# Two PSUM bank pairs of a hybrid encoder, each given to one part of the scan, and the bonus sums moved beside the key sums

## The chip, the cores and the metric

One core of a Trainium2 chip runs the whole program. The metric is the device time of one execution in microseconds (us). Engines are called by the names of the profile: PE (TensorE, matmuls), PEld (its weight loads), DVE (VectorE), ACT (ScalarE), POOL (GpSimd), SP (SyncE, which issues the DMAs). Each engine works through a queue of its own in order and meets the others at semaphores.

## The reference

Two encoder layers on 256 tokens of width 2048. Each projects its normed input to two groups of heads: 16 RWKV-7 heads of 64 (a delta-rule scan in both directions) and a windowed attention. Both are gated, joined, sent through an output projection and added to the residual. The change lies in the scan, of which this matters here:

```
kk = heads(k * k_k);  kk = kk * rsqrt(max(sum(kk * kk), 1e-24))     # sum over a head's 64: "key sums"
for d in (forward, reverse):
    decay = exp(-exp(-softplus(-(w0[d] + tanh(xw) @ decay_up[d])) - 0.5))
    a     = sigmoid(a0[d] + xa @ iclr_up[d])
    kd    = heads(k * (1 + (a - 1) * k_a))
    y     = y + wkv_scan(r, decay, kd, v, kk, a, reverse=d)
    bonus = bonus + sum(r * kd * r_k)                                # over a head's 64: "bonus sums"
out = norm(y) * lnx_g + lnx_b + bonus * v
```

`wkv_scan` steps a 64 by 64 state S over the tokens: S = S * decay - (S kk)(a kk) + v kd, output S r.

## The kernel before

**Tiling.** The 256 tokens lie in the free dimension, features on the 128 partitions; one scan step takes two heads (128 partitions) at a time, so there are 8 head pairs p in each layer. A projection tile `pm` (128 output columns by 256 tokens) sums 16 steps of contraction; each step is three matmuls, since fp32 weights and inputs are split into a high and a low part (L311 hi by high `XH`, L312 hi by low `XL`, L313 `lo` by high). ACT makes `hi` from the raw weights (L241), DVE makes `lo` (L243), SP loads them. The projections of both layers form one long stream of such steps on PE.

**Windows and slots.** The rest of the work is cut into Python generators, which the kernel runs in windows. A window has 64 projection steps in 11 slots (`SLOTS`); in each slot some generators go one `yield` further, and then PE gets that slot's projection steps. Window w holds the work of several head pairs at once: `scan_p` prepares p = w and p = w - 1, `scan_i` (the Gram products `pg` and a triangular solve by doubling: `pq`, `pd`, with `tt` and `tv` the parts of the inverse) works on p = w - 2 and w - 3, `scan_b` (the chunk recurrence `pcc`, `suv`, and the output `py`, normed to `ysq` and turned back by PE at L1043) on w - 3 and w - 4. `STAGE_P`, `STAGE_I` and `STAGE_B` list for each lag the slots in which a generator is taken on; the first half of `STAGE_P` is for p = w, the second for p = w - 1, and each half has the steps at the front of a slot (`[8]`, `[9]`) and those behind the other scans.

**What sets the order.** PE's order is the order of the program. On the other engines a scheduler places instructions by priority; those called through `PA` and `PV` stay in program order among themselves on ACT and DVE, whose remaining instructions it moves between them (`lo` gets a priority of its own, `scan_b` another). A wait of PE holds all the projection steps behind it.

**`scan_p`.** It squares the keys (`mf`, `sl` are high and low parts of the squares), sums them over each head by a matmul with `BONES` into `pk`, and keeps the sums as `kd` (ACT). `pza` (L691 to L693) is the low-rank product of decay and rate; ACT takes `th` and `FR` from it, and DVE prefix sums and products follow (`FR`, `pp`, `ip`, `kd` with the reciprocal, `th`, `mv`). The bonus is `km` (shown as `th`), split into high and low (`ip`), summed by `BONES` into `pbn` (L706), and multiplied with v to `bv` on DVE.

**PSUM.** 8 banks of 512 fp32 columns. `ps_main` holds two projection tiles, `ps_c` the recurrence's tiles, and `ps_w` two pairs of banks under one tag, "w". A `wpair(name)` takes the next pair in turn, and its first writer waits until the readers of the tile that had that pair before are done. All of `pk`, `pza`, `vt`, `pbn`, `pg`, `pt`, `pq`, `pd`, `pf`, `pn`, and in the attention windows `pscr`, `ppt` and `po`, go through these two pairs alternately.

Of the kernel before, what the change touches and what calls it, by code (L numbers as in the profile page):

```python
# [9 lines left out]
F32 = mybir.dt.float32  # L10
# [5 lines left out]
AF = mybir.ActivationFunctionType  # L16
# [5 lines left out]
T = 256  # L22
# [22 lines left out]

STAGE_P = (([8], [4, 5, 7, 10]), ([9], [0, 1, 2, 3, 4, 5, 6, 7, 8, 9]))
STAGE_I = (list(range(SLOTS)), [0, 1, 2, 3, 4])
# [86 lines left out]
def hybrid_trunk_kernel(ctx, tc, xT, wi, wv, wo, par, fing, dup, iup, sink, pos, cst, out):  # L134
# [14 lines left out]
    ps_c = pool("ps_c", 1, space=PSUM)  # L149
    ps_w = pool("ps_w", 2, space=PSUM)  # L150

    def wpair(name):

        return ps_w.tile([128, 2, 512], F32, tag="w", name=name)

    def wbank(name):
        return wpair(name)[:, 0]

# [47 lines left out]
    class Norm:  # L206


        def add(self, sums):

            self.ps = wpair("pr")
            pr = self.ps[:, :, 0:1]
# [228 lines left out]
    def queue_inputs(l):  # L441
# [56 lines left out]
        if l == 0:  # L498

            inproj(0, lambda pm: S.later(29, lambda: xw_evac(pm)), raws=first_w, bank=lambda: wbank("pm")[:, 0:T])  # L500
# [173 lines left out]
    def layer(l):  # L674
# [33 lines left out]


        def scan_p(p, t):  # L710
            K = t["k"]
# [23 lines left out]
            pz, pa = pza[:, 0], pza[:, 1]  # L735
# [39 lines left out]
            PV.tensor_tensor(BK8[:, :, 2, :], c8(km), IP8, op=ALU.mult)  # L775
            PA.activation(BK8[64:128, :, 0, :], BK8[64:128, :, 2, :], AF.Copy)
            yield

            R, VV = t["r"], t["v"]
# [15 lines left out]
            for h in range(2):  # L795
                for q in range(2):
# [15 lines left out]
            yield  # L812
# [5 lines left out]
        def scan_i(p, t):  # L818
# [9 lines left out]
            for d in range(2):  # L828
                pg = wpair("pg")
                for c in range(NC):  # L830
# [18 lines left out]

            pt2 = wpair("pt")  # L850
            pts = [pt2[:, h] for h in range(2)]
# [53 lines left out]
            for li, b in enumerate(LEVELS):  # L905
# [30 lines left out]
                yield  # L936
                pd = wpair("pd")
                for d, c, h in dch:
# [3 lines left out]
                yield  # L942
            pf = wpair("pf")
            turned = turn(pf[:, :, 256:384], LEVELS[-1])
# [13 lines left out]

            pn = wpair("pn")
            for d in range(2):  # L960
# [112 lines left out]
        def scores(j):  # L1073
            m, g = divmod(j, 4)
            t = L.tq[j]
            Sc = t["S"] = st("ge", [2, 2, 264], bufs=2) if j == 2 else st("mv", [2, 2, 264], bufs=3)
            ps2 = wpair("pscr")
            pss = [ps2[:, h] for h in range(2)]
# [27 lines left out]
        def flip(j):  # L1106
            t = L.tq[j]
            t["P"] = []
            pp2 = wpair("ppt")
            for h in range(2):  # L1110
# [8 lines left out]
        def values(j):  # L1119
            m, g = divmod(j, 4)  # L1120
            t = L.tq[j]
            po = wbank("po")[:, 0:T]
# [36 lines left out]

    idle = wbank("warm")  # L1160
    zeros = QF.rearrange("p d c j -> p (d c j)")
# [122 lines left out]
```

## Time and profile before

| | |
|---|---|
| median of 3 runs | 1176.88 us (1175.71 to 1177.16) |
| profiled execution, whole time | 1176.53 us |
| its span | 1174.8 us |
| granted TensorE clock, mean | 0.994 |
| ACT busy | 67% |
| HBM traffic over the span | 138 GB/s |

The span runs from the first to the last instruction of the trace; the time lies 1.7 us above it. Busy times of PE are those of pipelined matmuls: a matmul of 256 columns is reported with 0.28 us, while the next one starts 0.12 us after it. So a stall of PE is read from the gaps between starts and from the list of waits, not from the busy share.

### The profile page before, as it was taken

To read this page: it belongs to the slowest core of one execution; us is meant where nothing else is said; L and a number is where in the kernel's file an instruction comes from. 1 tells how busy PE (TensorE), PEld (TensorE's weight loads), DVE (VectorE), ACT (ScalarE), POOL (GpSimd) and SP (SyncE) were. 2 spreads that over 40 slices of the span, in tenths; PEclk is the share of its full clock that TensorE was granted. 3 is DMA by queue.
4 is the path that set the end of the run, shared out by engine and by line. 5 is a ranking of instruction groups with operands and counts; after the bars stand their busy time and mean duration, and the time that the engine had idled before them with its cause. 6 is when DMAs were issued, how large, how long until landed. Compare 5 with 4: busy or idle time off the path is not lost.

```text
span 1174.8 us, 38087 instructions
## 1 busy us (share of the span) xinstructions
PE 1148.4 (98%) x16151; PEld 1073.7 (91%) x16151; DVE 907.0 (77%) x2017; ACT 781.6 (67%) x1971; POOL 21.7 (2%) x23
## 2 busy tenths in 40 slices
PE   8999999999999999999999999999999999999996
PEld 6998999899899999899999889999999999899996
DVE  6899978888877677766678888978887767786654
ACT  6667867776875666645556677876786666675553
POOL 0000000000000000000000000000000000000000
PEclk8999999999999999999999999999999999999998
DMA  7544333333333443477655443333233344346653
GB/s 258 168 152 133 119 111 119 107 98 117 109 112 124 129 126 120 133 244 233 213 176 176 139 134 115 109 107 127 97 112 110 120 132 126 105 143 193 213 190 124
DMA packets 60410, 166.63 MB, mean 142 GB/s; under 512 B 7728, under 2 KB 22736, under 8 KB 60240
## 3 DMA queue, kind: packets, MB, share of 16 engines
q1 hardware_dynamic: 60240, 164.21, 43.4%
q8 instruction: 126, 2.06, 0.7%
q14 instruction: 44, 0.36, 0.1%
HBM read 157.37 MB, written 4.19 MB: 138 GB/s over the span
## 4 chain that ended last, share of the span: by engine, by line
PE 63%; DVE 15%; issue 14%; ACT 5%; DMA 2%; SPq 0%; POOL 0%; DVEq 0%; POOLq 0%; ACTq 0%
PE pm L311 15%; PE pm L313 13%; PE pm L312 13%; DVE lo L243 4%; PE pg L832 3%; PE pcc L995 2%; DVE kd L256 1%; ACT hi L241 1%; PE py L1007 1%; DVE th L256 1%; PE py L980 1%; PE pcc L1023 1%; PE pd L939 1%; DVE FR L256 1%; DVE mv L256 1%
## 5 line engine op out<-in xcount | busy, mean ns | idle before, releaser
L243 DVE TENSOR_TENSOR lo<-raw,hi 128x512 fp32r<-128x512 f32 x560 | 372.2, 687 | 112.9 <-ACT hi L241 107.3
L241 ACT ACTIVATE hi<-raw 128x512 fp32r<-128x512 f32 x560 | 329.6, 625 | 168.0 <-PE pm L312 95.2
L311 PE MATMUL pm<-XHa,hi 128*128 128x256 f32 x832 | 246.9, 297 | 1.9 <-ACT XHa L203 1.4
L311 PE MATMUL pm<-XHb,hi 128*128 128x256 f32 x832 | 243.2, 292 | 0.0
L313 PE MATMUL pm<-XHb,lo 128*128 128x256 f32 x832 | 233.8, 281 | 2.4 <-DVE lo L243 2.4
L313 PE MATMUL pm<-XHa,lo 128*128 128x256 f32 x832 | 234.2, 281 | 1.3 <-DVE lo L243 1.1
L312 PE MATMUL pm<-XLa,hi 128*128 128x256 f32 x832 | 234.3, 282 | 0.5 <-DVE XLa L204 0.3
L312 PE MATMUL pm<-XLb,hi 128*128 128x256 f32 x832 | 233.7, 281 | 0.0
L311 PEld LDWEIGHTS pm<-XHa,hi 128*128 128x128 f32 x832 | 157.0, 189 | 14.9 <-issue 3.2
L311 PEld LDWEIGHTS pm<-XHb,hi 128*128 128x128 f32 x832 | 157.0, 189 | 5.5
L313 PEld LDWEIGHTS pm<-XHb,lo 128*128 128x128 f32 x832 | 157.0, 189 | 3.2 <-DVE lo L243 3.2
L313 PEld LDWEIGHTS pm<-XHa,lo 128*128 128x128 f32 x832 | 157.3, 189 | 2.5 <-DVE lo L243 2.5
L312 PEld LDWEIGHTS pm<-XLa,hi 128*128 128x128 f32 x832 | 157.4, 189 | 1.1 <-DVE XLa L204 1.1
L312 PEld LDWEIGHTS pm<-XLb,hi 128*128 128x128 f32 x832 | 157.1, 189 | 0.3 <-DVE XLb L204 0.3
L1018 ACT ACTIVATE suv<-pcc 64x128 f32<-64x128 f32 x128 | 34.5, 270 | 72.3 <-PE pcc L1016 48.7
L311 PE MATMUL pm<-MHa,hi 128*128 128x256 f32 x256 | 72.0, 281 | 0.0
L313 PE MATMUL pm<-MHa,lo 128*128 128x256 f32 x256 | 71.9, 281 | 0.0
L312 PE MATMUL pm<-MLb,hi 128*128 128x256 f32 x256 | 71.8, 280 | 0.0
L311 PE MATMUL pm<-MHb,hi 128*128 128x256 f32 x256 | 71.7, 280 | 0.0
L313 PE MATMUL pm<-MHb,lo 128*128 128x256 f32 x256 | 71.7, 280 | 0.0
L312 PE MATMUL pm<-MLa,hi 128*128 128x256 f32 x256 | 71.7, 280 | 0.0
L311 PEld LDWEIGHTS pm<-MHa,hi 128*128 128x128 f32 x256 | 48.2, 188 | 0.8 <-issue 0.8
(292 smaller groups left out, 2317.3 us busy)
## 6 DMA issues: line engine op xcount, KB each, us to landing
raw<-wi SPq DMA_DIRECT2D x207, 512.0 KB
raw<-wo SPq DMA_DIRECT2D x64, 512.0 KB
raw<-wv SPq DMA_DIRECT2D x8, 512.0 KB
rrot<-u SPq DMA_DIRECT2D x80, 32.0 KB
vg<-xT SPq DMA_DIRECT2D x16, 128.0 KB
xd<-vg SPq DMA_DIRECT2D x16, 128.0 KB
vg<-xd SPq DMA_DIRECT2D x16, 128.0 KB
g<-dup SPq DMA_DIRECT2D x16, 97.0 KB
```

Source lines behind the costliest of these rows:

```text
L241: A.activation(hi[:, q], raw[:, q], AF.Copy)
L243: V.tensor_tensor(lo[:, q], raw[:, q], hi[:, q].bitcast(F32), op=ALU.subtract)
L256: return lambda *a, **k: tc.keep_in_program_order(getattr(self.engine, name)(*a, **k))
L311: PE.matmul(pm, wh, rh[:, kk, :], start=(kk == 0), stop=False)
L312: PE.matmul(pm, wh, rl[:, kk, :], start=False, stop=False)
L313: PE.matmul(pm, wl, rh[:, kk, :], start=False, stop=(kk == 15))
L832: PE.matmul(pg[:, h, c * 128 : (c + 1) * 128], BK[half[h], d, c, 1 - h : 3 - h, :].rearrange("p s j -> p (s j)"), MV[half[h], d, c].rearra ...
L939: PE.matmul(narrow(pd[:, d], h, c), hx(TT, d, c, h), sub(QF, h ^ d, d, c, d * b), start=True, stop=True)
L980: PE.matmul(py[half[h], c, :], GE[h][:, d, c, 1, :], SUV[:, d, c, h, :], start=(i == 0 and d == 0), stop=(i >= NC // 2), skip_group_check= ...
L995: PE.matmul(pc[half[h], 0, d, :], GE[h][r, d, ci[d], 0, :], SUV[r, d, ci[d], h, :], start=True, stop=True)
L1007: PE.matmul(py[half[h], ci[d], :], MV[half[h], d, ci[d], 1, :], SUV[half[h], d, ci[d], h, :], start=False, stop=False, skip_group_check=True,)
L1018: A.activation(here(h), pc[half[h], 1], AF.Copy)
```

## The change

`ps_w` has two tags of one pair each instead of one tag of two. The argument `side` says which: side 1 ("wx") for `pr`, `pg`, `pt`, the solver's `pq` of levels under 5 and `pd` of levels under 4, `pscr` and the warm-up; side 0 ("wy") for the new tile `sums`, `pza`, `vt`, the later `pq` and `pd`, `pf`, `pn`, `ppt`, `po` and the first `pm`. A tile of one tag always follows the one of the same tag before it.

`sums` is one pair for two sums: the bonus sums of p - 1 go to its side 0 and the key sums of p to its side 1, both at the front of slot 8. So the bonus matmuls are moved from slot 9 to slot 8 (`STAGE_P`, and a `yield` more ahead of them). The bonus arithmetic on DVE (`km`'s sum and its product with r) is moved from slot 6 to slot 5, its split into `ip` from slots 7 and 8 to slot 6; `MV`'s first products and `PC` come behind the copies of `vt`, in slot 7, its last product (R times `PP`) in slot 8; `kkr` (ACT) goes from slot 7 to slot 9. Lines from L835 on carry numbers that are 8 higher than before.

```diff
...
 
 SLOTS = 11
 
-STAGE_P = (([8], [4, 5, 7, 10]), ([9], [0, 1, 2, 3, 4, 5, 6, 7, 8, 9]))
+STAGE_P = (([8], [4, 5, 9, 10]), ([8], [0, 1, 2, 3, 4, 5, 6, 7, 8, 9]))
 STAGE_I = (list(range(SLOTS)), [0, 1, 2, 3, 4])
 STAGE_B = (list(range(5, SLOTS)), [i for i in range(SLOTS) if i != 7], [7])
 ATT = [
...
     dram = pool("dram", 1, space=bass.MemoryType.DRAM)
     ps_main = pool("ps_main", 2, space=PSUM)
     ps_c = pool("ps_c", 1, space=PSUM)
-    ps_w = pool("ps_w", 2, space=PSUM)
-
-    def wpair(name):
-
-        return ps_w.tile([128, 2, 512], F32, tag="w", name=name)
-
-    def wbank(name):
-        return wpair(name)[:, 0]
+    ps_w = pool("ps_w", 1, space=PSUM)
+
+    def wpair(name, side):
+
+        return ps_w.tile([128, 2, 512], F32, tag="wx" if side else "wy", name=name)
+
+    def wbank(name, side):
+        return wpair(name, side)[:, 0]
 
     def st(tag, shape, dt=F32, bufs=1):
         return sp.tile([128, *shape], dt, tag=tag, name=tag, bufs=bufs)
...
 
 
 
+        banks = {}
+
+        def sums(w, side):
+
+            if w not in banks:
+                banks[w] = wpair("sums", 0)
+            return banks[w][:, side]
+
         def scan_p(p, t):
             K = t["k"]
             two = lambda x: x.unsqueeze(1).to_broadcast([128, 2, T])
...
             yield
             PV.tensor_tensor(square[1], sq, square[0].bitcast(F32), op=ALU.subtract)
             yield
-            KR = st("kkr", [T])
-            PA.activation(KR, K, AF.Identity, scale=prm(P_KK, p))
-            yield
-            pk = wbank("pk")
+            pk = sums(p, 1)
             head_sums(pk, square)
             KD = st("kd", [T])
             A.activation(KD, pk[:, 0:T], AF.Copy)
             yield
+            KR = st("kkr", [T])
+            PA.activation(KR, K, AF.Identity, scale=prm(P_KK, p))
+            yield
 
             iu, du = t["iu"], t["du"]
-            pza = wpair("pza")
+            pza = wpair("pza", 0)
             pz, pa = pza[:, 0], pza[:, 1]
             for d in range(2):
                 low_rank(pz[:, d * T : (d + 1) * T], [a[0 : RANK + 1, d, :] for a in du], [a[0 : RANK + 1] for a in L.TW])
...
             PV.tensor_tensor(dd(km), dd(km), two(K), op=ALU.mult)
             PV.tensor_tensor(BK8[:, :, 2, :], c8(km), IP8, op=ALU.mult)
             PA.activation(BK8[64:128, :, 0, :], BK8[64:128, :, 2, :], AF.Copy)
-            yield
-
             R, VV = t["r"], t["v"]
-            MV = st("mv", [2, NC, 2, 64], bufs=3)
-            kr4 = c4(KR)
-            PV.scalar_tensor_tensor(MV[:, 0, :, 0, 1:64], PP[:, 0, :, 0:63], -1.0, kr4[:, :, 1:64], op0=ALU.mult, op1=ALU.mult)
-            PV.scalar_tensor_tensor(MV[:, 1, :, 0, 0:63], PP[:, 1, :, 1:64], -1.0, kr4[:, :, 0:63], op0=ALU.mult, op1=ALU.mult)
-            PA.activation(MV[:, 0, :, 0, 0:1], kr4[:, :, 0:1], AF.Copy, scale=-1.0)
-            PA.activation(MV[:, 1, :, 0, 63:64], kr4[:, :, 63:64], AF.Copy, scale=-1.0)
-            PC = st("pc", [2, NC], bufs=3)
-            PA.activation(PC[:, 0, :], PP[:, 0, :, 63], AF.Copy)
-            PA.activation(PC[:, 1, :], PP[:, 1, :, 0], AF.Copy)
+            PV.tensor_tensor(km[:, 0:T], km[:, 0:T], km[:, T : 2 * T], op=ALU.add)
+            PV.scalar_tensor_tensor(km[:, 0:T], km[:, 0:T], prm(P_RK, p), R, op0=ALU.mult, op1=ALU.mult)
+            yield
+
+            bonus = high(km[:, 0:T], "ip")
+            low(bonus, km[:, 0:T])
             SUV = st("suv", [2, NC, 2, 64], bufs=3)
-            vt = wpair("vt")
+            vt = wpair("vt", 0)
             for b in range(2):
                 for q in range(2):
                     for h in range(2):
...
                         pick(SUV, half[1 - h], q * 128 + h * 64, [NC * 128, 2], [256, 2], [1, 64]),
                         vt[half[q], h, 0:128].rearrange("p (b x) -> p b x", b=2).unsqueeze(1).to_broadcast([64, 2, 2, 64]), AF.Copy,
                     )
-            PV.tensor_tensor(km[:, 0:T], km[:, 0:T], km[:, T : 2 * T], op=ALU.add)
-            PV.scalar_tensor_tensor(km[:, 0:T], km[:, 0:T], prm(P_RK, p), R, op0=ALU.mult, op1=ALU.mult)
+            yield
+            MV = st("mv", [2, NC, 2, 64], bufs=3)
+            kr4 = c4(KR)
+            PV.scalar_tensor_tensor(MV[:, 0, :, 0, 1:64], PP[:, 0, :, 0:63], -1.0, kr4[:, :, 1:64], op0=ALU.mult, op1=ALU.mult)
+            PV.scalar_tensor_tensor(MV[:, 1, :, 0, 0:63], PP[:, 1, :, 1:64], -1.0, kr4[:, :, 0:63], op0=ALU.mult, op1=ALU.mult)
+            PA.activation(MV[:, 0, :, 0, 0:1], kr4[:, :, 0:1], AF.Copy, scale=-1.0)
+            PA.activation(MV[:, 1, :, 0, 63:64], kr4[:, :, 63:64], AF.Copy, scale=-1.0)
+            PC = st("pc", [2, NC], bufs=3)
+            PA.activation(PC[:, 0, :], PP[:, 0, :, 63], AF.Copy)
+            PA.activation(PC[:, 1, :], PP[:, 1, :, 0], AF.Copy)
+            yield
+            pb = sums(p + 1, 0)
+            head_sums(pb, [bonus[:, i] for i in range(2)])
             yield
             PV.tensor_tensor(MV[:, :, :, 1, :], c4(R).unsqueeze(1).to_broadcast([128, 2, NC, 64]), PP, op=ALU.mult)
             t.update(BK=BK, MV=MV, PC=PC, SUV=SUV)
-            bonus = high(km[:, 0:T], "ip")
-            yield
-            low(bonus, km[:, 0:T])
-            yield
-            pb = wbank("pbn")
-            head_sums(pb, [bonus[:, i] for i in range(2)])
             yield
             t["bv"] = bv = st("bv", [T], bufs=3)
             PV.tensor_tensor(bv, pb[:, 0:T], VV, op=ALU.mult)
...
             GE = [GE[:, h] for h in range(2)]
             GEd = lambda d: pick(GE[0], every, d * NC * 128, [2 * NC * 128, 2], [128, NC], [1, 128])
             for d in range(2):
-                pg = wpair("pg")
+                pg = wpair("pg", 1)
                 for c in range(NC):
                     for h in range(2):
                         PE.matmul(
...
                 sub = lambda x, r, d, c, o: pick(x, half[r], d * T + c * 64 + o, [2 * b, 32 // b], [1, b])
                 narrow = lambda o, r, c: o[half[r], c * 32 : (c + 1) * 32]
                 flat4 = lambda x: x.rearrange("p d (n b) -> p d n b", b=b)
-                pq = wpair("pq")
+                pq = wpair("pq", li < 5)
                 if li in (1, 3):
                     (low_rows, key_rows)[li // 2]()
                 if li == 0:
...
                 if turned:
                     turned()
                 yield
-                pd = wpair("pd")
+                pd = wpair("pd", li < 4)
                 for d, c, h in dch:
                     PE.matmul(narrow(pd[:, d], h, c), hx(TT, d, c, h), sub(QF, h ^ d, d, c, d * b), start=True, stop=True)
                 with tc.high_priority(offset=PRIO_TC):
                     V.copy_predicated(t_sub(TC), t_mask, flat4(pd[:, :, 0:128]))
                 yield
-            pf = wpair("pf")
+            pf = wpair("pf", 0)
             turned = turn(pf[:, :, 256:384], LEVELS[-1])
             o = lambda d, c, h: pf[half[h ^ d], d, c * 64 : (c + 1) * 64]
             for d in range(2):
...
```

The sides of the tiles that are not shown are those named above.

More of the change, by code (lines that the diff above doesn't have):

```diff
@@ L209, in add @@
         def add(self, sums):
-            self.ps = wpair("pr")
+            self.ps = wpair("pr", 1)
             pr = self.ps[:, :, 0:1]
@@ L498, in queue_inputs @@
         if l == 0:
-            inproj(0, lambda pm: S.later(29, lambda: xw_evac(pm)), raws=first_w, bank=lambda: wbank("pm")[:, 0:T])
+            inproj(0, lambda pm: S.later(29, lambda: xw_evac(pm)), raws=first_w, bank=lambda: wbank("pm", 0)[:, 0:T])
             inproj(1, lambda pm: S.later(13, lambda: xa_evac(pm)))
@@ L776, in scan_p @@
             PA.activation(BK8[64:128, :, 0, :], BK8[64:128, :, 2, :], AF.Copy)
+            R, VV = t["r"], t["v"]
+            PV.tensor_tensor(km[:, 0:T], km[:, 0:T], km[:, T : 2 * T], op=ALU.add)
+            PV.scalar_tensor_tensor(km[:, 0:T], km[:, 0:T], prm(P_RK, p), R, op0=ALU.mult, op1=ALU.mult)
             yield
-            R, VV = t["r"], t["v"]
-            MV = st("mv", [2, NC, 2, 64], bufs=3)
-            kr4 = c4(KR)
-            PV.scalar_tensor_tensor(MV[:, 0, :, 0, 1:64], PP[:, 0, :, 0:63], -1.0, kr4[:, :, 1:64], op0=ALU.mult, op1=ALU.mult)
-            PV.scalar_tensor_tensor(MV[:, 1, :, 0, 0:63], PP[:, 1, :, 1:64], -1.0, kr4[:, :, 0:63], op0=ALU.mult, op1=ALU.mult)
-            PA.activation(MV[:, 0, :, 0, 0:1], kr4[:, :, 0:1], AF.Copy, scale=-1.0)
-            PA.activation(MV[:, 1, :, 0, 63:64], kr4[:, :, 63:64], AF.Copy, scale=-1.0)
-            PC = st("pc", [2, NC], bufs=3)
-            PA.activation(PC[:, 0, :], PP[:, 0, :, 63], AF.Copy)
-            PA.activation(PC[:, 1, :], PP[:, 1, :, 0], AF.Copy)
+            bonus = high(km[:, 0:T], "ip")
+            low(bonus, km[:, 0:T])
             SUV = st("suv", [2, NC, 2, 64], bufs=3)
-            vt = wpair("vt")
+            vt = wpair("vt", 0)
             for b in range(2):
@@ L848, in scan_i @@
                 PA.activation(flat(AB[half[h]]), GE[h][half[h]].rearrange("p d c s j -> p (d c) s j")[:, :, 0, :], AF.Copy)
-            pt2 = wpair("pt")
+            pt2 = wpair("pt", 1)
             pts = [pt2[:, h] for h in range(2)]
@@ L957, in scan_i @@
             yield
-            pn = wpair("pn")
+            pn = wpair("pn", 0)
             for d in range(2):
@@ L1076, in scores @@
             Sc = t["S"] = st("ge", [2, 2, 264], bufs=2) if j == 2 else st("mv", [2, 2, 264], bufs=3)
-            ps2 = wpair("pscr")
+            ps2 = wpair("pscr", 1)
             pss = [ps2[:, h] for h in range(2)]
@@ L1108, in flip @@
             t["P"] = []
-            pp2 = wpair("ppt")
+            pp2 = wpair("ppt", 0)
             for h in range(2):
@@ L1121, in values @@
             t = L.tq[j]
-            po = wbank("po")[:, 0:T]
+            po = wbank("po", 0)[:, 0:T]
             for kb in range(2):
@@ L1158, in hybrid_trunk_kernel @@
     V.memset(QF, 0.0)
-    idle = wbank("warm")
+    idle = wbank("warm", 1)
     zeros = QF.rearrange("p d c j -> p (d c j)")
```

## The prediction

> **What bounds the kernel now.** I read the page first, then the waits of TensorE, then the busy time by stage, and last the timelines of three places. The page shows a core on which TensorE is nearly always busy:
>
> ```profile
> span 1174.8 us, 38087 instructions
> PE 1148.4 (98%) x16151; PEld 1073.7 (91%) x16151; DVE 907.0 (77%) x2017; ACT 781.6 (67%) x1971; POOL 21.7 (2%) x23
> ```
>
> With 98% on PE, only what PE waits for can move the time. The list of PE's waits (line, what it waited for, microseconds in total, times, longest) names those that the change touches:
>
> ```profile
> PE pm L313 <- DVE lo L243: 3.5, 7, 1.2
> PE pza L691 <- DVE bv L256: 3.3, 9, 0.7
> PE pbn L706 <- DVE ip L256: 2.4, 3, 1.1
> PE pd L939 <- ACT tt L901: 1.8, 1, 1.8
> ```
>
> `pza` is the low-rank product that starts a scan window, `bv` the VectorE product that reads the bonus sums `pbn` out of PSUM, `ip` the low half of the bonus. The `pza` and `pbn` waits together are 5.7 us, 0.5% of the span: that is all that PE could win here. The last, on `tt`, has no step of the change in front of it.
>
> By stage (length, busy time and count of each engine, granted clock, DMA share, GB/s) a steady window of layer 2, and the stretch in layer 1 in which the second window's scan begins (w=1):
>
> ```profile
> 766.60:806.90 40.30, 39.97 (x760) 37.05 (x752) 34.04 (x72) 30.25 (x82) 1.31 (x1) 1.00 0.34 112
> 59.00:80.00 21.00, 19.58 (x173) 18.90 (x172) 19.69 (x40) 15.34 (x36) 0.00 (x0) 1.00 0.49 158
> ```
>
> In the steady window VectorE has 6 us to spare in 40; at w=1 it is busy 19.69 of 21.00 us, so there a wait of PE for VectorE is as long as VectorE's queue ahead of it. The granted clock is 1.00 in both.
>
> **The change at w=1 of each layer.** VectorE and TensorE around this place in layer 2 (start, duration, engine, line, operation; in brackets idle time and its releaser):
>
> ```profile
> 648.11 0.28 PE L706 MATMUL pbn<-ip,BONES 128*128 128x256 f32 x1
> 649.48 0.39 PE L706 MATMUL pbn<-ip,BONES 128*128 128x256 f32 x1 [1.09 <-DVE ip L256]
> 651.72 0.28 PE L313 MATMUL pm<-XHb,lo 128*128 128x256 f32 x1
> 651.84 0.28 PE L691 MATMUL pza<-TW,duh 97*128 97x256 f32 x1
> ```
>
> ```profile
> 649.01 0.42 DVE L256 TENSOR_TENSOR ip<-th,ip 128x256 fp32r<-128x256 f32 x1
> 649.34 0.42 DVE L453 TENSOR_TENSOR u<-pm,rb 128x256 f32<-128x256 f32 x1
> 649.68 1.74 DVE L256 RECIPROCAL kd<-kd 128x256 f32<-128x256 f32 x1
> 651.34 0.39 DVE L455 SCALAR_TENSOR_TENSOR kr<-u,PR,kr 128x255 f32<-128x255 f32 x1
> 651.93 0.69 DVE L243 TENSOR_TENSOR lo<-raw,hi 128x512 fp32r<-128x512 f32 x1 [0.20 <-ACT hi L241]
> 652.54 0.48 DVE L456 SCALAR_TENSOR_TENSOR kr<-u,PR,kr 128x255 f32<-128x255 f32 x1
> 652.93 0.41 DVE L256 TENSOR_TENSOR bv<-pbn,vg 128x256 f32<-128x256 f32 x1
> 655.61 0.42 DVE L464 TENSOR_TENSOR g<-pm,rb 128x256 f32<-128x256 f32 x1 [1.32 <-PE pm L313]
> ```
>
> And one group on ScalarE, the copies of the window's values:
>
> ```profile
> 642.91 1.55 ACT L797 ACTIVATE suv<-vt 64x256 f32<-64x256 f32 x4
> ```
>
> The place at `pza` in layer 1, cut to four rows:
>
> ```profile
> 72.67 0.28 PE L706 MATMUL pbn<-ip,BONES 128*128 128x256 f32 x1
> 74.05 0.39 PE L706 MATMUL pbn<-ip,BONES 128*128 128x256 f32 x1 [1.09 <-DVE ip L256]
> 76.41 0.28 PE L691 MATMUL pza<-TW,duh 97*128 97x256 f32 x1
> 77.50 0.41 DVE L256 TENSOR_TENSOR bv<-pbn,vg 128x256 f32<-128x256 f32 x1
> ```
>
> PE starts `pza` at 651.84, a full microsecond before `bv` begins to read `pbn` (652.93 to 653.34). It may, because `pza` stands in the pair that the key sums `pk` had, and `pbn` in the other one. The change takes that freedom away: the sums of keys and bonus and `pza` are three tenants of one pair. In TensorE's queue, layer 1, w=1, before:
>
> ```order
> L311 MATMUL pm<-XHb,hi 128x256
> L312 MATMUL pm<-XLb,hi 128x256
> L313 MATMUL pm<-XHb,lo 128x256
> L691 MATMUL pza<-TW,duh 128x256
> L692 MATMUL pza<-acc,duh 128x256
> ```
>
> and now:
>
> ```order
> L313 MATMUL pm<-XHb,lo 128x256 [waits DVE_49]
> L311 MATMUL pm<-XHb,hi 128x256
> L312 MATMUL pm<-XLb,hi 128x256
> L313 MATMUL pm<-XHb,lo 128x256
> L691 MATMUL pza<-TW,duh 128x256 [waits DVE_49]
> L692 MATMUL pza<-acc,duh 128x256
> ```
>
> `DVE_49` is VectorE's semaphore: `pza` has gained a wait for VectorE, and what it waits for is `bv`. In VectorE's queue `bv` has not moved up. Layer 1, w=1, the difference on VectorE (minus before, plus now):
>
> ```order
> -L243 TENSOR_TENSOR lo<-raw,hi 128x512 x3
> -L256 TENSOR_TENSOR ip<-th,ip 128x256
> +L243 TENSOR_TENSOR lo<-raw,hi 128x512 x2
>  L453 TENSOR_TENSOR u<-pm,rb 128x256
>  L256 RECIPROCAL kd<-kd 128x256
> ```
>
> The bonus's `ip` is made earlier, but the splitting steps `lo` and the two `mv` products take its place, so the same work stands ahead of `u`, the 1.74 us reciprocal and `bv`. In the rows VectorE has one gap, 0.20 us, between `ip` and `bv`, so `bv` ends where it did. So three things happen. The `pbn` wait goes (649.48 − 648.11 less one matmul interval of 0.12: 1.25 us), since `ip` now ends some two microseconds before PE needs it. PE then comes to `pza` at 651.84 − 1.25 = 650.59. There it stands until `bv` is done at 652.93 + 0.41 = 653.34, plus 0.05 us (`ip` ended at 649.43, its matmul started at 649.48) and 0.1 us for a first matmul after a wait (0.39 instead of 0.28): the program behind `pza` runs 1.65 us later than before. In layer 1 it is 77.91 + 0.15 − 76.41 = 1.65 as well. The low half of the bonus may now wait for ScalarE, which makes the high half in the neighbourhood of the four copies; I put a gap of 0.3 us on VectorE ahead of `bv` for it, a fifth of their 1.55 us, against the one of 0.2 at 651.93 that goes: +0.1. Together **2 × 1.75 = +3.5 us**, in which the gain on `pbn` is contained. Everything behind `pza` on PE waits with it, the projection matmuls too, and the scan of the window, which starts from `pza`. The lower bound is what VectorE could take back later: PE's waits for `lo` (3.5 us in the whole run) lie partly after this place, and I allow 2.0 of them; the upper one is the whole wait, 2 × 3.0 us, if the 1.25 us were lost elsewhere.
>
> **At w=2.** The two directions of the Gram product `pg` now share one pair, so the second must wait until VectorE has read the first (`ge`). Layer 2:
>
> ```profile
> 657.75 1.22 DVE L838 TENSOR_TENSOR ge<-pg,C 128x1024 f32<-128x1024 f32 x1
> 658.55 1.16 PE L832 MATMUL pg<-mv,FR 64*128 64x128 f32 x16
> ```
>
> The first `ge` ends at 658.97, the second `pg` begins at 658.55: 0.47 us with the release. Later windows leave more room, since `ge` comes sooner there. The Trainium skill, "Perfetto Trace Analysis", section "Optimizing Tensor Performance", has the rule that independent groups of matmuls should rotate through PSUM banks, so that reading one result overlaps the next matmuls; this change does the reverse for `pg`. By that rule each of the two layers' 8 windows could pay 0.47, 14 more than here, and the sum below would be 6.6 us higher. Next, the solver's second `pq` meets the first one's reader `tt` and may lose another 0.1 us. VectorE, which is not held by this, gives back about 0.25 of it in the next waits for `lo`. For both layers **+0.65 us** (0 to 1.2).
>
> **The steady windows.** With the bonus arithmetic a slot earlier, the order on VectorE around `ysq` (the scan output, scaled by its deviation) changes. Layer 2, from the product `FR` on, before:
>
> ```order
> L256 TENSOR_TENSOR FR<-th,ip 128x8x64
> L256 TENSOR_TENSOR sl<-t_14321,mf 128x256
> L455 SCALAR_TENSOR_TENSOR vg<-u,PR,vg 128x255
> L243 TENSOR_TENSOR lo<-raw,hi 128x512
> L456 SCALAR_TENSOR_TENSOR vg<-u,PR,vg 128x255
> L256 TENSOR_TENSOR ysq<-py,yv 128x256
> ```
>
> and now:
>
> ```order
> L256 TENSOR_TENSOR FR<-th,ip 128x8x64
> L243 TENSOR_TENSOR lo<-raw,hi 128x512
> L256 TENSOR_TENSOR th<-th 128x256
> L455 SCALAR_TENSOR_TENSOR vg<-u,PR,vg 128x255
> L256 SCALAR_TENSOR_TENSOR th<-th,PR,kr 128x256
> L256 TENSOR_TENSOR sl<-t_14310,mf 128x256
> L456 SCALAR_TENSOR_TENSOR vg<-u,PR,vg 128x255
> L256 TENSOR_TENSOR ysq<-py,yv 128x256
> ```
>
> Two `th` steps now stand ahead of `ysq`. What they take, who waits for `ysq`, and the wait for `bv` behind:
>
> ```profile
> 790.15 0.42 DVE L256 TENSOR_TENSOR ysq<-py,yv 128x256 f32<-128x256 f32 x1
> 791.74 0.42 DVE L256 TENSOR_TENSOR th<-th 128x256 f32<-128x256 f32 x1
> 792.08 0.45 DVE L941 CAST_PREDICATED tv<-LV,pd 128x256 f16<-128x256 uint8 x1
> 792.41 0.48 DVE L256 SCALAR_TENSOR_TENSOR th<-th,PR,kr 128x256 f32<-128x256 f32 x1
> 792.81 0.59 DVE L1025 TENSOR_TENSOR suv<-pcc,pc 64x128 f32<-64x128 f32 x2
> 790.82 0.66 PE L1043 MATMUL py<-C,ysq 64*64 64x64 f32 x16
> 802.26 0.39 PE L691 MATMUL pza<-TW,duh 97*128 97x256 f32 x1 [0.34 <-DVE bv L256]
> ```
>
> From start to start the two `th` take 792.08 − 791.74 = 0.34 and 792.81 − 792.41 = 0.40 us (the durations overlap). VectorE is full here, so `ysq` ends at 790.57 + 0.74 = 791.31 and `py`, which began at 790.82, waits about 0.55 us. Ahead of `bv` VectorE's work is the same, so `bv` keeps its time; PE comes to `pza` later by 0.55 and the old wait of 0.40 (0.34 in the row, and the slower first matmul) disappears: net +0.15 per window, four windows in layer 2, +0.6. In layer 1:
>
> ```profile
> 174.90 0.42 DVE L256 TENSOR_TENSOR ysq<-py,yv 128x256 f32<-128x256 f32 x1
> 175.38 0.33 PE L1043 MATMUL py<-C,ysq 64*64 64x64 f32 x4
> 186.91 0.39 PE L691 MATMUL pza<-TW,duh 97*128 97x256 f32 x1 [0.40 <-DVE bv L256]
> ```
>
> `ysq` would end at 175.32 + 0.74 = 176.06, against 175.38: +0.72 with the release, less the 0.47 of `pza`: +0.25, in two windows of this layer (in the others the order differs less), +0.5. Together **+1.1 us** (0, if `ysq` stays early, to 3.6, if `pza` gives nothing back: 4 × 0.55 + 2 × 0.72).
>
> **At nothing.** No instruction is added or taken away, and no DMA is moved on SP's queue, nor anything on POOL's. The `pbn` matmuls move beside `pk`, a change of place in PE's stream at the same price. The key scaling `kkr` and the `mv` and `pc` steps move on ScalarE, which idles a third of the time and has them ready before `bv`. In the attention part all pairs still alternate where PE waited before.
>
> **Sum** against the profiled execution, 1176.53 us (0.35 below the median of the runs, 1176.88): 1176.53 + 3.5 + 0.65 + 1.1 = **1181.8 us**. A difference within 0.2%, 2.35 us, can't be told from no change in this kernel.
>
> **The rivals.** *Faster* (0.08): `bv` could come early enough, because the bonus is ready earlier. Then 2.5 us of `pbn` and the 3.3 us of `pza` waits go: 1176.5 − 5.8 = 1170.7. It decides if `bv` ends before 650.6 in layer 2, 2.7 us earlier; for it speaks that `ip` is early, against it the reciprocal and four other steps that still stand ahead of it.
> *No difference to be told* (0.20): the loss at w=1 is taken back by the waits for `lo` behind it (2.0 us as allowed above) and the steady windows cost nothing: 1176.53 + 3.5 − 2.0 + 0.65 = 1178.7, in a span of 1177.5 to 1179.2. For it speaks that VectorE has spare time in the mean; against it that the scan behind `pza` feeds VectorE, which idles 1.3 us for PE right after.
> *Dearer* (0.12): `bv` slips as `ysq` does and `pza` gives nothing back: 3.6 in place of 1.1, 1184.3 us.
> *The clock* (0.08): PE now stands still some 3.0 us in one piece (650.59 to 653.5) twice. The start of the run shows the granted clock (the last but two figure) falling to 0.50 after a stretch in which PE was often idle:
>
> ```profile
> 5.00:10.00 5.00, 3.81 (x15) 2.11 (x13) 2.36 (x5) 2.34 (x5) 0.00 (x0) 0.93 0.95 308
> 10.00:15.00 5.00, 4.22 (x17) 3.58 (x17) 4.08 (x10) 4.66 (x12) 0.00 (x0) 0.50 1.02 404
> ```
>
> Five microseconds at half clock would cost 2.5 us, two of them 5.0: 1186.8. The longest wait with the clock at 1.00 is the 1.8 us of the `pd` row, so the trace leaves 3.0 open. The Trainium skill, "TensorE: Matmul & The Clock Gate", section "HAM oscillation", puts the gap that drops the clock above about 3.4 us: by that rule this rival just fails, and no run here shows it yet.
>
> **The numbers.** My forecast has what is left, 0.52, with a range of its own from 1179.9 to 1183.7. The range of 1177.8 to 1185.0 leaves out the faster case, the clock and the low end of the second rival, together about 0.2. Slower by over 0.2% are forecast, dearer and clock: 0.72; same 0.20; faster 0.08.
>
> **What would show it.** Right: in PE's waits `pbn` falls from 2.4 us to near nothing, and `pza` for `bv` has two waits of about 3 us, near 75 and 651, while those of 0.4 go; a new wait of `py` for `ysq` of 0.5 to 0.7 us six times; one of 0.4 us of `pg` at w=2; a steady window of 40.45 instead of 40.30 us. Wrong: `bv` starts earlier than 652.9 at w=1, PE's waits for `lo` after 655 vanish, or the granted clock falls below 1.00 there.

## The result and the profile after

The changed kernel took 1183.86 us in the median of 5 runs (1182.57 to 1187.34), the kernel before 1175.71 us in the median of 5: a ratio of 1.0067, 95% interval 1.0052 to 1.0082. It is slower, by some 8 us where 5.25 were forecast; 1183.86 lies within the range of 1177.8 to 1185.0 and just above 1183.7, the upper end of the forecast's own. The profiled execution after took 1184.25 us. Its page and its list of what PE waited for:

```profile
span 1182.4 us, 38104 instructions
PE 1149.5 (97%) x16151; PEld 1075.7 (91%) x16151; DVE 907.5 (77%) x2017; ACT 782.4 (66%) x1971; POOL 21.7 (2%) x23
```

```profile
PE pza L691 <- DVE bv L256: 7.1, 4, 3.1
PE py L1051 <- DVE ysq L256: 3.3, 7, 0.7
PE pm L313 <- DVE lo L243: 2.2, 3, 1.2
PE pd L947 <- ACT tt L909: 1.7, 1, 1.7
PE po L1134 <- ACT ip L1125: 1.4, 4, 0.4
PE pg L840 <- DVE ge L846: 0.8, 2, 0.4
```

The instruction counts of the compute engines are those of before and the busy times nearly so. The wait of the bonus sums for `ip`, 2.4 us before, has left the list; `pza` for `bv` has two waits of 3.1 us in place of many small ones, `py` for `ysq` and `pg` for `ge` are new. New too are the four of `po` for `ip` in the attention windows. They stand in the lists of all ten profiles here with split pairs and of none of the four with the pairs in turn. They cost the span nothing: such a `po` tile is 0.3 to 0.5 us later against before than the tile ahead of it, and the next tile is back at the old distance.

**w=1.** PE and VectorE in layer 2 (start, duration, engine, line, operation, idle before and its releaser):

```profile
652.67 0.28 PE L313 MATMUL pm<-XHb,lo 128*128 128x256 f32 x1
656.09 0.39 PE L691 MATMUL pza<-TW,duh 97*128 97x256 f32 x1 [3.14 <-DVE bv L256]
```

```profile
647.42 0.43 DVE L256 TENSOR_TENSOR ip<-th,ip 128x256 fp32r<-128x256 f32 x1 [0.61 <-ACT ip L256]
652.66 1.74 DVE L256 RECIPROCAL kd<-kd 128x256 f32<-128x256 f32 x1
655.62 0.42 DVE L256 TENSOR_TENSOR bv<-sums,vg 128x256 f32<-128x256 f32 x1
```

PE comes to `pza` and stands 3.42 us from start to start, 3.3 more than a matmul interval, until `bv` ends at 655.62 + 0.42 = 656.04. The reciprocal stands ahead of `bv` as it did. The gap on VectorE for ScalarE's half of `ip` is 0.61 us (0.42 in layer 1).

**w=2 and the steady windows.** First the second `pg` of layer 2 behind the first `ge`; then, in a steady window, `ysq` and `py`, and `pza` without a wait; then the window as a whole (length, busy time and count of PE, PEld, DVE, ACT and POOL, granted clock, DMA share, GB/s):

```profile
663.61 1.22 DVE L846 TENSOR_TENSOR ge<-pg,C 128x1024 f32<-128x1024 f32 x1
664.88 0.49 PE L840 MATMUL pg<-mv,FR 64*128 64x128 f32 x4 [0.40 <-DVE ge L846]
```

```profile
797.41 0.42 DVE L256 TENSOR_TENSOR ysq<-py,yv 128x256 f32<-128x256 f32 x1
797.88 0.68 PE L1051 MATMUL py<-C,ysq 64*64 64x64 f32 x16 [0.32 <-DVE ysq L256]
808.99 0.38 PE L691 MATMUL pza<-TW,duh 97*128 97x256 f32 x1
```

```profile
773.13:813.62 40.49, 40.17 (x760) 37.23 (x752) 34.05 (x72) 30.34 (x82) 1.31 (x1) 1.00 0.35 110
```

The window is 40.49 us long, against 40.30.

**The clock.** Microseconds 656 to 661, right behind the wait of layer 2 (the clock is the last figure but two), and a stretch of 8 us in layer 1:

```profile
656.00:657.00 1.00, 0.91 (x6) 0.91 (x7) 0.97 (x3) 0.00 (x0) 0.00 (x0) 0.87 0.01 4
657.00:658.00 1.00, 1.00 (x7) 1.00 (x6) 0.00 (x0) 0.00 (x0) 0.00 (x0) 0.50 0.55 61
658.00:659.00 1.00, 1.00 (x7) 1.00 (x6) 0.00 (x0) 0.46 (x1) 0.00 (x0) 0.50 0.70 270
660.00:661.00 1.00, 1.00 (x10) 1.00 (x9) 0.00 (x0) 0.00 (x0) 0.00 (x0) 0.93 0.00 0
...
302.00:310.00 8.00, 8.00 (x114) 7.51 (x116) 7.07 (x15) 6.85 (x21) 0.00 (x0) 0.80 0.36 122
```

From 656.8 to 660.2 PE has half its clock. Three of its matmuls there, which start every 0.21 us instead of every 0.12:

```profile
657.67 0.41 PE L691 MATMUL pza<-XA,iuh 96*128 96x256 f32 x1
657.88 0.41 PE L692 MATMUL pza<-rrot,iuh 96*128 96x256 f32 x1
658.09 0.41 PE L693 MATMUL pza<-XA,iu 96*128 96x256 f32 x1
```

Over the 8 us from 654 to 662 the mean is 0.79, so 0.21 x 8 = 1.7 us of work are lost. From 302 to 310 0.20 x 8 = 1.6 us are lost as well; the clock fell there half a microsecond behind the wait of `pd` for `tt`, 1.7 us in the list. Before, the same `pd` waited as long, and the clock stayed up:

```profile
302.00:310.00 8.00, 8.00 (x145) 7.33 (x146) 7.72 (x17) 7.47 (x20) 0.00 (x0) 1.00 0.22 68
```

So this execution had two half-clock stretches, together 3.3 us.

**Where the 7.7 us of span lie.** The first matmul of `pg` or `pza` in each window marks the same place in both programs. How much later it comes after, and what each stretch added:

| stretch | added, us | forecast |
|---|---|---|
| start, up to w=0 | -0.2 | 0 |
| w=1, layer 1 / layer 2 without its half clock | +1.75 / +2.0 | +1.75 / +1.75 |
| half clock in layer 2 (w=1) and in layer 1 (at 302) | +1.7 and +1.6 | 0 |
| w=2 and w=3, both layers | +0.7 | +0.65 |
| w=4 to w=7, layer 2: 0.22, 0.20, 0.24, 0.24 | +0.9 | +0.6 |
| w=4 to w=7, layer 1: 0.32, -0.72, 0.22, and -0.2 without the half clock | -0.4 | +0.5 |
| rest (0.8 us back between layer 1's last `pg` and layer 2's first `pza`, 0.5 lost at the end) | -0.35 | 0 |

The sum is 7.7. What was forecast comes to 4.95 here where the sum had 5.25; the clock is the difference.

### The profile page after: what moved, and what is told of

The parts are those of the page before. It is cut to its first block, busy times and chain, and to the rows that moved or that the text cites. A ratio compares the mean times of both kernels' runs of the same rounds, so it can differ in the third digit from the quotient of the medians.

```text
span 1182.4 us, 38104 instructions
## 1 busy us (share of the span) xinstructions
PE 1149.5 (97%) x16151; PEld 1075.7 (91%) x16151; DVE 907.5 (77%) x2017; ACT 782.4 (66%) x1971; POOL 21.7 (2%) x23
## 4 chain that ended last, share of the span: by engine, by line
PE 69%; issue 14%; DVE 10%; ACT 5%; DMA 1%; SPq 0%; POOL 0%; POOLq 0%; DVEq 0%; ACTq 0%
PE pm L311 17%; PE pm L312 14%; PE pm L313 14%; DVE lo L243 4%; PE pg L840 3%; PE pcc L1003 2%; PE pcc L1031 2%; PE py L1015 1%; DVE FR L256 1%; PE py L988 1%; PE pd L947 1%; DVE th L256 1%; ACT hi L241 1%; PE pcc L1021 1%; PE pq L938 1%
```

## The experiments

My theory: the loss is `pza`'s wait for `bv` at w=1, caused by the shared pair and by `bv`'s late place on VectorE; the idle stretch sometimes halves the clock on top; small waits of `pg` and `py` make up the rest. The main rival: the moved order loads VectorE or ScalarE differently, and the pair only shows where that is collected. Ratios are to the kernel before, run on the same chip beside it; edits are against the changed kernel where nothing else is said.

**`pza` of w=1 on the other pair.** The wait alone is taken away.

```diff
-            pza = wpair("pza", 0)
+            pza = wpair("pza", int(p == 1))
```

> The changed kernel with one edit: the pza of the second window of each layer (p = 1) takes the other pair (side 1), so that it no longer follows the sums. Theory (the wait for bv at w=1 is the main loss, and the gap of 3.3 us it makes in the work of PE also drops the clock in some runs): both waits of 3.3 us go, PE's list shows pza for bv at 0.0 to 0.6 us, the granted clock stays at 0.994, and the time falls by 5 to 8 us against the changed kernel (1183.9), to 1176 to 1179; the lower end if nothing behind pza was waiting for VectorE anyway. Rival (the moved order on VectorE and ScalarE is the loss, and the pair only shows where it is collected): PE waits as long behind pza, for lo or pg, and the time stays above 1181.

1175.01 us, ratio 0.9983 (0.9975 to 0.9992): 0.84 points below the changed kernel's 1.0067, and faster than before. PE's list:

```profile
PE py L1051 <- DVE ysq L256: 3.8, 7, 0.7
PE pza L691 <- DVE bv L256: 0.8, 2, 0.6
```

No wait of that size took its place. The rival falls: with the order as changed and only one tile in another pair, the loss is gone. One thing differs from what I expected: the profiled execution has a half-clock stretch about 300 too, so such stretches don't come from w=1 alone.

**The wait filled.** PE multiplies an idle tile while it waits. The tile `zeros` is cleared once, at the start of the program; in layer 1 it holds zeros, in layer 2 also what the solver of layer 1 left in it.

```diff
             pz, pa = pza[:, 0], pza[:, 1]
+            if p == 1:
+                fill = wbank("fill", 1)
+                for _ in range(14):
+                    PE.matmul(fill, zeros[:, 0:128], zeros, start=True, stop=True)
```

> The changed kernel with 14 matmuls of 512 columns on zeros put ahead of the pza of w=1 in each layer, into the other pair, which nothing uses then: 14 x 0.22 us = 3.1 us of work that fills most of the 3.3 us in which PE waits there. Theory (the stall itself costs some 1.7 to 2.1 us a layer, and on top the idle stretch halves the clock for 3.4 us in some executions, 1.6 us each): pza starts where it did, the half-clock stretch behind it is gone, clock 0.994 in nearly every run, time 1182.0 to 1182.8 with a narrow scatter, so 1 to 2 us below the changed kernel's median. Rival (the clock moves by chance and has nothing to do with this wait): the scatter from 1182.6 to 1187.3 stays, and the time is that of the changed kernel or a little above.

1181.19 us (1180.47 to 1182.00), ratio 1.0034 (1.0021 to 1.0046). Three microseconds of added matmuls make the kernel faster by 0.33%, and the runs lie within 1.5 us of each other. The eight microseconds that hold the end of the wait in layer 2:

```profile
653.00:661.00 8.00, 7.65 (x65) 6.58 (x63) 4.84 (x11) 2.79 (x6) 0.00 (x0) 1.00 0.27 78
```

The clock stays at 1.00 here, and no half-clock stretch is left between 30 and 1150. PE comes to the fill at 650.58 and `pza` starts at 653.79, so the wait itself is still there. The time is about a microsecond better than I expected; the two stretches of the changed kernel's profile, which are gone here, were 3.3 us together.

**The changed kernel again**, beside the three that follow.

> The changed kernel once more, beside the kernel before and the three below. Theory: 1182 to 1185 us with a scatter of some microseconds; the executions with a mean granted clock near 0.994 lie at 1182 to 1183, those near 0.990 one or two half-clock stretches (1.6 us each) above. Rival (the difference between this kernel and the one with the filled wait was one between two sessions on the chip): the median comes within 0.8 us of the 1181.2 of the filled wait.

1184.87 us (1184.46 to 1186.36), ratio 1.0067 (1.0051 to 1.0082). The mean clock was 0.990 or 0.991 in all six runs, and the time 1184.5 to 1186.4; in the first series the one run at 0.994 took 1182.57 and the one at 0.989 took 1187.34. The ratio is that of the first series, so the distance to the filled wait is not one between sessions. In this profile half-clock stretches lie behind both waits of w=1 and at 302.

**A longer wait.** Two reciprocals ahead of the first `bv`; their results are overwritten.

```diff
             t["bv"] = bv = st("bv", [T], bufs=3)
+            if p == 0:
+                for _ in range(2):
+                    PV.reciprocal(bv, VV)
             PV.tensor_tensor(bv, pb[:, 0:T], VV, op=ALU.mult)
```

> The changed kernel with two reciprocals of 128x256 (1.74 us each, results overwritten) on VectorE ahead of the bv of p = 0, in each layer. They lengthen the wait of pza at w=1 by up to 3.4 us a layer, to about 6.7 us. Theory (an idle stretch of PE of this length halves the clock for 3.4 us, and at 3.3 us it does so only sometimes): both layers show the half clock behind pza in the profiled execution and the mean clock is at or under 0.991 in every run; time = changed without a drop (1182.6) + 6.7 + 2 x 1.6 = 1191 to 1193.5. Rival (the drops are chance): 1189 to 1190 in runs with clock 0.994, and such runs are there.

1194.76 us (1193.59 to 1195.29), ratio 1.0145 (1.0128 to 1.0162), with a mean clock of 0.984 to 0.986 in every run. The wait; then layer 1 from 70 to 94 and the middle piece in layer 2. `pza` starts at 80.73 and at 664.73:

```profile
PE pza L691 <- DVE bv L256: 15.8, 5, 7.2
```

```profile
70.00:78.00 8.00, 3.48 (x28) 3.27 (x28) 8.00 (x13) 3.03 (x7) 0.00 (x0) 0.94 0.38 132
78.00:86.00 8.00, 5.27 (x24) 5.27 (x25) 2.93 (x5) 1.32 (x3) 0.00 (x0) 0.50 0.19 66
86.00:94.00 8.00, 7.64 (x72) 7.04 (x71) 5.91 (x9) 2.98 (x6) 0.00 (x0) 0.92 0.27 82
662.00:670.00 8.00, 5.27 (x24) 5.28 (x25) 2.67 (x4) 1.33 (x3) 0.00 (x0) 0.50 0.20 66
```

Each wait grew by about 4 us, not 3.4, since a `lo` and the second `kd` step came between the reciprocals and `bv`; the time is a microsecond above my range. The half clock came in both layers and lasted some 10 us, not 3.4: by the means of 0.94 and 0.92 it began at 78 − 0.06 x 8 / 0.5 = 77.0 and ended at 86 + 0.08 x 8 / 0.5 = 87.3. But 3.7 us of this lie in the wait, where PE had nothing to do; 6.5 us lie behind `pza`, some 3.3 us of lost work. Here the clock fell while PE still stood, some 3.6 us into the wait. So at both places of this profile a longer idle stretch brought the half clock, and more of it behind the wait; the rival of chance falls for these places.

**The pairs alone**, in the order of before; the edit is against the kernel before.

```diff
-    ps_w = pool("ps_w", 2, space=PSUM)
+    ps_w = pool("ps_w", 1, space=PSUM)
...
-        return ps_w.tile([128, 2, 512], F32, tag="w", name=name)
+        return ps_w.tile([128, 2, 512], F32, tag="wx" if side else "wy", name=name)
...
-            pk = wbank("pk")
+            pk = wbank("pk", 0)
...
-            pb = wbank("pbn")
+            pb = wbank("pbn", 0)
```

> The kernel before with the two tags of one pair each (the sides as in the change, pk and pbn both on side 0), with its own slots and order. Theory (the pairs cause the wait at w=1 and that of pg): pbn still waits 1.25 us for ip at w=1, pza then 1.6 us for bv, pg 0.5 us for ge at w=2; ysq does not wait and the steady windows keep 40.3 us: before + 2 x 1.65 + 2 x 0.5 = +3.5 to +5 us, 1180.5 to 1182. Rival (the losses need the moved order): no wait at w=1 over 0.5 us and a time within 1 us of before.

1180.95 us, ratio 1.0029 (1.0017 to 1.0041).

```profile
PE pza L691 <- DVE bv L256: 6.2, 11, 1.4
PE pbn L706 <- DVE ip L256: 2.3, 3, 1.1
PE pg L832 <- DVE ge L838: 0.8, 2, 0.4
```

`pza` waits 1.4 us for `bv` behind the old 1.1 us for `ip`: the stall of w=1 is there in two pieces, `pg` waits for `ge`, and the steady windows keep 40.3 us. Behind the two pieces the clock stays at 1.00 in both layers. In the profile the program is 4.2 us behind before at the end of w=3 of layer 2, 1.4 of it the stretch at 302 with half its clock. Both waits come from the pairs and need no moved order.

**The order alone**, with the pairs in turn.

```diff
-    ps_w = pool("ps_w", 1, space=PSUM)
+    ps_w = pool("ps_w", 2, space=PSUM)
...
-        return ps_w.tile([128, 2, 512], F32, tag="wx" if side else "wy", name=name)
+        return ps_w.tile([128, 2, 512], F32, tag="w", name=name)
```

> The changed kernel with ps_w as before: two pairs under one tag, taken in turn; the shared sums tile, the slots and the order as changed. Theory (pairs by part of the scan cause the w=1 wait and the pg wait, the order causes the ysq waits): pza at w=1 does not wait for bv, pg at w=2 does not wait for ge, ysq waits stay; time = before + 1 to 2 for ysq - 2.5 for the bonus wait that is gone = 1174.5 to 1177.5. Rival (sharing one pair between the two sums is what costs, whatever the tags): pza still waits about 3 us at w=1 and the time is 1180 or more.

1175.95 us, ratio 0.9991 (0.9982 to 1.0000).

```profile
PE py L1051 <- DVE ysq L256: 3.6, 7, 0.7
PE pza L691 <- DVE bv L256: 1.3, 3, 0.6
```

The tile that both sums share costs nothing by itself: the next tile, `pza`, takes the other pair. The waits for `ysq` come with the order, and its gain on the old bonus wait about pays for them. The pairs alone (+0.29%) and the order alone (−0.09%) don't add up to the change (+0.67%). An estimate of the 5.5 us between: the order's gain of 2.5 us on the bonus wait is lost again where the pairs are split, since PE then comes to `pza` earlier and waits there in one piece, and the two half-clock stretches of the profile are 3.3 us.

**The bonus products back in slot 6.**

```diff
             R, VV = t["r"], t["v"]
+            yield
+
             PV.tensor_tensor(km[:, 0:T], km[:, 0:T], km[:, T : 2 * T], op=ALU.add)
             PV.scalar_tensor_tensor(km[:, 0:T], km[:, 0:T], prm(P_RK, p), R, op0=ALU.mult, op1=ALU.mult)
-            yield
-
             bonus = high(km[:, 0:T], "ip")
```

> The changed kernel with the two bonus products (th, the sum and its product with r) put back from slot 5 to slot 6; pairs and all else as changed. Theory (the two th steps ahead of ysq cost 0.55 to 0.75 us in seven windows, of which 0.4 come back at pza): the waits of py for ysq, 3.3 us in the list, go; pza waits for bv by about 0.4 us in the steady windows again; each steady window of layer 2 goes from 40.50 back to 40.3 us, together -1 to -1.6 us. Rival (the steady windows are longer for the pairs' sake, not for the order): the windows stay at 40.5 us. The waits at w=1 stay in both.

1192.29 us, ratio 1.0127 (1.0111 to 1.0142). A miss:

```profile
PE pza L691 <- DVE bv L256: 7.6, 11, 2.1
PE sums L706 <- ACT ip L256: 4.3, 7, 1.2
PE sums L706 <- DVE ip L256: 2.8, 4, 0.7
```

The waits for `ysq` went and those of `pza` came back, as expected, but a step later in the chain had no room: the sums in slot 8 now wait 7.1 us for `ip`. In this order the sums in slot 8 need the products in slot 5. In this profile the clock fell behind the wait of 2.1 us of `pza` in layer 2 too, for 3.4 us; in layer 1, behind 2.0 us, it did not.

**`pg` in turn on both pairs**, beside `pza` on the other pair.

```diff
-            pza = wpair("pza", 0)
+            pza = wpair("pza", int(p == 1))
...
-                pg = wpair("pg", 1)
+                pg = wpair("pg", 1 - d)
```

> The changed kernel with the pza of p = 1 on the other pair (as run before, 1175.0 us) and pg in turn on both pairs (side 1 - d). Theory: the two waits of pg for ge, 1.2 us in the list, go, and nothing takes their place, since the other pair holds a pza that ScalarE has read long before: 1173.5 to 1174.8 us, 0.2% below the kernel before. Rival: VectorE has the later products in front of it anyway and pq waits instead: 1175.0 us as without the edit.

1191.54 us, ratio 1.0119 (1.0103 to 1.0136), against 0.9983 without the second line. Also a miss:

```profile
PE pg L840 <- ACT tt L909: 14.8, 14, 1.1
```

My expectation took in `pza` in that pair and not the solver's late `pq`, which has it at that place: two waits of together 1.2 us were exchanged for 14 of up to 1.1.

**`bv` early on VectorE.** Pairs and slots as changed.

```diff
-            PV.tensor_tensor(bv, pb[:, 0:T], VV, op=ALU.mult)
+            with tc.high_priority(offset=PRIO_TC):
+                V.tensor_tensor(bv, pb[:, 0:T], VV, op=ALU.mult)
```

> The changed kernel with one edit: bv on VectorE is given a high priority and taken out of the fixed order of its neighbours, so that it stands behind the first mv instead of behind the reciprocal (w=1), and ahead of MLa and the reciprocal in the steady windows. Pairs, slots and arithmetic as changed. Theory (it is not the shared pair as such that costs, but that bv, the reader which frees it, stands late in VectorE's queue): the waits of pza for bv, 7.1 us, fall under 1 us, the clock stays near 0.994 and the time is that of the kernel with pza on the other pair or less, 1173 to 1176 us; py still waits for ysq (3 to 5 us in all, 0.55 to 0.9 each, now with nothing given back at pza). Rival (VectorE as a whole is behind at w=1 and any order of it costs the same): PE waits for lo or g in place of bv, time over 1180 us.

1172.43 us, ratio 0.9969 (0.9958 to 0.9981). At w=1 of layer 2:

```profile
644.27 0.42 DVE L823 TENSOR_TENSOR bv<-sums,vg 128x256 f32<-128x256 f32 x1
646.91 0.28 PE L691 MATMUL pza<-TW,duh 97*128 97x256 f32 x1
647.07 1.74 DVE L256 RECIPROCAL kd<-kd 128x256 f32<-128x256 f32 x1
```

`bv` is done two microseconds before PE needs the pair, and no wait of `pza` for it is left in the list. The mean clock is 0.995 to 0.997 in all six runs. So the shared pair costs nothing once its last reader no longer stands behind the long reciprocal.

**`bv` early, and `ysq` ahead of the second `th`.** The lower priority puts one `th` behind `ysq`.

```diff
-            PV.tensor_tensor(km[:, 0:T], km[:, 0:T], km[:, T : 2 * T], op=ALU.add)
-            PV.scalar_tensor_tensor(km[:, 0:T], km[:, 0:T], prm(P_RK, p), R, op0=ALU.mult, op1=ALU.mult)
+            with tc.high_priority(offset=-20):
+                V.tensor_tensor(km[:, 0:T], km[:, 0:T], km[:, T : 2 * T], op=ALU.add)
+                V.scalar_tensor_tensor(km[:, 0:T], km[:, 0:T], prm(P_RK, p), R, op0=ALU.mult, op1=ALU.mult)
```

> The same, and the two th products get a lower priority, by which ysq stands behind one of them, where it stood in time before the change. Theory (each of the two th ahead of ysq made PE wait): the waits of py for ysq fall from over 3 us to under 1 us, and since pza no longer waits there, the steady windows of layer 2 come down from 40.5 to 39.9 or 40.0 us; 1170 to 1173 us. Rival: the sums then wait for the later ip, as they did when the products stood in slot 6 (7 us), and the time is above that of the kernel with bv early alone.

1174.56 us, ratio 0.9984 (0.9975 to 0.9992): not better than `bv` early alone.

```profile
PE pm L313 <- DVE lo L243: 3.6, 6, 0.7
PE sums L706 <- ACT ip L256: 1.1, 2, 0.6
```

No wait for `ysq` is left. In layer 2's steady windows one for `lo` of about 0.7 us stands in its place and they grow to 40.8 us; in layer 1 the windows do get shorter. The cause is one step back: ScalarE now makes its half of `ip` behind all four copies of `vt`, where with `bv` early alone it came between them, and VectorE stands 0.87 us in front of its own half (790.67 in this profile), with the `lo` steps behind it.

**The same with both pairs in turn, and `bv` early with both pairs in turn** (one tag "w" and 2 buffers, as in the order alone).

> The same again, but with both pairs under one tag, in turn, as before the change. Theory (the pairs by part of the scan are of no use here and cost the waits of pg at w=2): pg's two waits (0.8 us) go, 0.5 to 1.5 us under the kernel ahead. Rival (with bv early the split pairs cost nothing and save waits of pq and pd): same time or above.

> The kernel with bv early (the th products where the change has them), with both pairs under one tag, in turn, as before the change. Theory (the pairs cost two waits of pg for ge, 1.1 us together, and two of pq, 0.5 us, and give nothing back here): these go, 0.5 to 1.5 us below the 1172.4 of bv early: 1171 to 1172 us. Rival (the split saves as much elsewhere): 1172.4 or more.

1172.67 us, ratio 0.9974 (0.9963 to 0.9986), and 1171.63 us, ratio 0.9963 (0.9949 to 0.9977). The waits of `pg` for `ge` are gone in both. The second is the fastest in the median, but its interval overlaps that of `bv` early with the split pairs, so whether the split costs its 1 us of `pg` waits there is left open.

## Why the prediction was right, and where it was too small

**w=1** was right in mechanism and place: the wait for `ip` went, PE came to `pza` early and stood until `bv`. The two layers lost 1.75 and 2.0 us, against 1.75 each; most of the 0.25 is the gap for ScalarE's `ip`, 0.61 us in layer 2 against 0.42 in layer 1, where I put 0.3. The bound that VectorE might take 2 us back was hardly used: of PE's waits for `lo` behind these places 0.3 us went in layer 1 and 0.2 in layer 2. That 0.2 was the only such wait after 655, so by the letter a sign of being wrong, that these waits vanish, came true; it is too small to matter. That the pairs cause it is shown by the pairs alone (the waits appear) and by `pza` on the other pair (they vanish); that it is `bv`'s place in the queue is shown by `bv` early.

**w=2** was right: 0.40 us in the list for each of the two `pg`, 0.7 us over w=2 and w=3 with the `pq` waits. The Trainium skill ("Perfetto Trace Analysis", section "Optimizing Tensor Performance") has independent groups of matmuls rotate through PSUM banks. My price for that rule, a wait in all sixteen windows, did not come: PE's list has two, and with `pg` on both pairs in turn, 14 waits of up to 1.1 us.

**The steady windows** of layer 2 grew by 0.20 to 0.24 us where I had 0.15, by the exchange described: `py` waits 0.5, `pza` no longer 0.4. In layer 1 I expected +0.5 from two windows and the windows gave back 0.4. `py` waits there in three windows, seven times in all where I had six. In w=5 `pza` had waited 0.76 us before, the bonus sums a third time for `ip` (0.2 us in the list, 0.4 with the slower start) and `pcc` for `suv` (0.2); all three went, against 0.7 for `ysq`, and I had left them out. So it is partly luck that the stretches I had forecast come to 4.95 us where I had 5.25: a gain of 0.9 us against my layer 1 hides that the other terms were 0.6 too small.

**At nothing** I had put the attention part, with all pairs still alternating where PE waited before. They don't: `po` waits 1.4 us for `ip`, which the next tiles give back.

**The clock** is the term that failed: I put nothing for it in the sum and gave its rival 0.08, and the sign of being wrong that I had named, a granted clock below 1.00 behind this wait, is there. By the rows above a half-clock stretch behind a 3.3 us wait costs 1.6 to 1.7 us, less than the 2.5 that I had for it from the start of the run, but it came in both profiles of the changed kernel, and its mean clock was 0.989 to 0.992 in ten of eleven runs. The mean can't place the stretches: it also holds the half clock at the start and the end of a run, 7.2 us of lost work in the profile before and 6.6 in the one after. The filled wait shows the part that hangs on idle time: matmuls during the same wait keep the clock up and take 0.33% off, some 3.9 us, about two stretches; whether that at 302 is one of them is not shown. My reading that 3.0 us might just be short enough was wrong in size, too: PE stood 3.3 us. The page "TensorE: Matmul & The Clock Gate" of the Trainium skill puts the limit above some 3.4 us in section "HAM oscillation"; here waits of 3.3 us met the half clock in one layer in one profile and in both in another, and one of 2.1 us met it with the products in slot 6. The `pd` wait of 1.7 to 1.8 us near 300 is in all fourteen profiles, the half clock behind it in six, of which the one before is none. What decides between them is not settled.

**The faster rival** named its own condition, that `bv` ends 2.7 us earlier. The change didn't meet it; `bv` early does, and is faster than before by 0.31%.

## What to carry to other kernels

When buffers are divided among the parts of a program, list for each buffer who reads it last and what stands ahead of that reader in its engine's queue: a tile may be ready early and its buffer still come free late. Mend such a wait at the reader's place in the queue before the buffers are dealt out anew. And price a new idle stretch of PE of 2 to 3 us or more above its length, since the clock can drop behind it.

## What was not expected of the hardware

Half-clock stretches of about 3.4 us, each 1.6 to 1.7 us of lost work, came behind three of four waits of 3.3 us, one of two near 2 us and six of fourteen near 1.8 us. With a wait of 7.2 us some 10 us were at half clock, 6.5 of them behind it. A kernel with 28 more matmuls, put where PE would have stood, ran 0.33% faster than the one without them.
